# A staging place moved by 1088 words at the seam between an MLP's up and down projections

## The chip, the cores and the metric

The program runs on one core of one Trainium2 chip, as one launch. The metric is the device time in microseconds of one execution; the number compared is the median of several runs.

## The reference

The reference is one inference step of a two-layer hybrid decoder. It serves a prompt of 1024 tokens and a sample group of 8 x 8 = 64 tokens with shared weights, 1088 tokens in all, in float32. Layer 0 mixes tokens with a diagonal state-space model, layer 1 with attention over shared keys and values; both also attend to a memory. What matters here is the MLP that ends each layer:

```
def sqrelu_mlp(x, w_up, w_down):
    h = jax.nn.relu(x @ w_up)
    return (h * h) @ w_down
...
    h = h + sqrelu_mlp(rmsnorm(h, p["norm_mlp"][i]), p["w_up"][i], p["w_down"][i])
```

`x` has 1024 features (D_MODEL) and the hidden layer has 4096 (D_FF), so `w_up` is 1024 x 4096 and `w_down` 4096 x 1024.

## The kernel before, in words

The 1088 tokens are cut into four column chunks of 272 (`CN`). Every product is made of three float32r matmuls, on a high and a low half of each operand. `split(H, L, src)` makes such halves: the scalar engine writes the rounded high half (line 221), then the vector engine, or GpSimd, writes the difference (line 222).

**Strassen-like products.** The MLP multiplies 2 x 2 blocks with seven products instead of eight. `seven` (lines 428 to 455) runs them in order on TensorE, each into one of three pairs of PSUM banks in turn, so a product can start only when the readers of the product three places earlier are through. After product 4 it calls `out(1, 1, p, u4)` and then, on line 449, adds the same bank to `u2`; that line is the bank's last reader. `out` is given by the caller. In the up projection it is line 578 and squares the rectified sum; in the down projection it adds into the accumulator `H5` (line 627 for the first of the seven blocks of hidden features, 629 and 630 for later ones).

**The up projection.** `mlp` walks over sixteen pairs of up tiles in the order 14, 0 to 13, 15. Each leaves four results `q[m][n]` (hidden tile m, token half n). For tiles 0 to 13, `to_hidden` forms the seven operands that the down projection will need, splits each into a staging place and writes it to the DRAM scratch tensors `hops`. Tiles 14 and 15 belong to the eighth block of hidden features, which is multiplied in the conventional way at the end: there the four results are split as they are, in the order (0,0), (1,1), (0,1), (1,0), into the places of the list `hl4`, and written half by half to the scratch tensor `hcnv` (32 transfers over both layers). The transfers out of `hcnv`'s staging and the operand loads are tied into one issue order on SyncE's queue by `load_on`.

**The storage.** All of this lives in `setA`, four places of 2176 words (per partition). A ring of ten temporaries of 544 words (`tmps`) uses

```
((3, 0), (2, 0), (1, 1), (3, 1), (2, 1), (1, 2), (1, 3), (3, 2), (3, 3), (1, 0))
```

where (i, j) is words 544j to 544j + 543 of place i. Three staging places of 1088 words (`hl`) are the upper half of place 2 and the two halves of place 0. For the last tile the list `hl4` names four places, with the fourth outside that ring.

**The seam.** When the last up tile (15) is computed, the first down weights and the first four operands of block 0 are loaded; the other three operand loads are issued behind the first staged result (`late`). Then the down projection starts. Its accumulator `H5` covers all of `setA`:

```
H5 = joined(setA).at([128, 2, 2, 8, CN])
...
h = H5[:, :, n, 4 * d + 2 * e + m, :]
```

so that token half n and row r of the output lie at words 272r of places n and n + 2. The first down pair (block 0, d = 0) runs its two seven-product sequences interleaved and writes rows 0 to 3, words 0 to 1087 of every place; the second (d = 1) writes words 1088 to 2175. The down projection then goes on through blocks 1 to 6, with weights split on the fly into the eight places `wr`, which come free as TensorE finishes with them.

**The order of the work.** The source gives the engines and the traced order; the compiler's scheduler orders each engine's queue from the dependencies and a timing model, and derives the semaphore waits from which words overlap. So moving a place changes the waits, and can change the order on the queues.

Of the kernel before, what the change touches and what calls it, by code (L numbers as in the profile page):

```python
# [48 lines left out]
def yoco_step(ctx: ExitStack, tc: tile.TileContext, I, O, upto=99, dbg=None):  # L49
# [116 lines left out]
    setA = [top.words(n) for n in CW]  # L166
# [44 lines left out]
    def mm3(out, aH, aL, bH, bL, first, last):  # L211
        mm(out, aH, bH, first, False)
        mm(out, aH, bL, False, False)
        mm(out, aL, bH, False, last)
# [21 lines left out]
    def flush():  # L236
        while later:
            tick()
# [148 lines left out]
    def xop(i, g):  # L387
        return xplace[g][i].at([128, 2, 4, CN], F32R)
# [38 lines left out]
    def seven(lhs, rhs, nk, gs, tmp, out):  # L427

        s1, u2, u4 = (t[:, gs] for t in tmp)

        def product(i):
            n = turn["bank"] = (turn["bank"] + 1) % 3
            v = shaped(banks[:, 1024 * n:1024 * n + 1024], [128, 2, 512], F32)[:, :, 0:CN]
            for g in range(gs.start, gs.stop):
                for k in range(nk):
                    mm3(v[:, g], *lhs(i, k), *rhs(i, g, k), k == 0, k == nk - 1)
            return v[:, gs]

        S.activation(s1, product(0), AF.Copy)
        yield  # L440
        V.tensor_tensor(u2, product(1), s1, op=ALU.add)
        yield
        out(0, 0, product(2), s1)
        yield
        V.tensor_tensor(u4, product(3), u2, op=ALU.add)
        yield
        p = product(4)
        out(1, 1, p, u4)
        V.tensor_tensor(u2, p, u2, op=ALU.add)
        yield  # L450
        out(0, 1, product(5), u4)
        yield
        out(1, 0, product(6), u2)
        yield

    def by_turns(*seqs):
        for _ in zip(*seqs):
            tick()
# [45 lines left out]
    def mlp(l, hs, done, each=None):  # L504
# [6 lines left out]
        hl = Ring([setA[i].sub(1088 * j, 1088) for i, j in ((2, 1), (0, 0), (0, 1))])  # L511
        hl4 = [hl.p[i] for i in (0, 1, 2, 0)]
        late = []

        def up_weights(j, more=False):
            return weight_ops((I["w_up"][l, 2 * j:2 * j + 2].rearrange("m p k f -> p m k f"), [2, 8, 128]),
                              lambda r: (r[:, 0, 0:4], r[:, 0, 4:8], r[:, 1, 0:4], r[:, 1, 4:8]), [4, 128], more)
# [10 lines left out]
        def to_hidden(j, q):  # L528
            b, kp = j // 2, j % 2

            def put(i, x):
                t = hl([128, 2, 2, CN], F32R)
                split(t[:, 0], t[:, 1], x)
                SY.dma_start(out=hops[i][b][:, kp], in_=t.rearrange("p h g n -> p h (g n)").bitcast(F32))

            if b < 7:
                operands(q[0][0], q[0][1], q[1][0], q[1][1], tmps(sh), put)
                return
            for (m, n), place in zip(((0, 0), (1, 1), (0, 1), (1, 0)), hl4):
                t = place.at([128, 2, 2, CN], F32R)  # L540
                split(t[:, 0], t[:, 1], q[m][n])
                to = hcnv[2 * kp + m].rearrange("p h (g n x) -> p h g n x", g=2, n=2)
                for i in range(2):
                    load_on(to[:, i, :, n], t[:, i].bitcast(F32))
                if late:
                    load_operands(late.pop(0))

        def down_weights(b, d):
            return weight_ops((I["w_down"][l, b, 2 * d:2 * d + 2].rearrange("i p k f -> p i k f"), [2, 4, 256]),
                              lambda r: tuple(r[:, :, k:4:2, 128 * m:128 * m + 128] for m in range(2) for k in range(2)),  # L550
                              [2, 2, 128])

        def next_operands(b):

            t = [hring([128, 2, 2, 2 * CN], F32R) for _ in range(7)]
            r = [t[i] for i in (0, 5, 1, 6, 2, 3, 4)] if b == 0 else t

            def load(which):
                for i in which:
                    load_on(r[i].bitcast(F32), hops[i][b])  # L560

            return r, load
# [4 lines left out]
        for n, j in enumerate(jorder):  # L567
            take = tmps if n else first
            tmp = [take(sh) for _ in range(3)]
            q = [[take(sh) for _ in range(2)] for _ in range(2)]  # L570

            for gs in (slice(0, 1), slice(1, 2)) if n < 2 else (slice(0, 2),):
                if n == 0 and gs.start:
                    continue

                def out(m, n, ps, u):
                    x = q[m][n][:, gs]
                    V.tensor_tensor(x, ps, u, op=ALU.add)  # L578
                    S.activation(x, x, AF.Relu)  # L579
                    S.activation(x, x, AF.Square)  # L580

                by_turns(seven(lambda i, k: (W[i][:, 0, k, :], W[i][:, 1, k, :]),
                               lambda i, g, k: (xop(i, g)[:, 0, k, :], xop(i, g)[:, 1, k, :]), 4, gs, tmp, out))
            if n == 0:

                flush()
                for m, c in ((1, 0), (0, 0), (1, 1), (0, 1)):
                    turn["bank"] = (turn["bank"] + 1) % 3
                    ps = banks[:, 1024 * turn["bank"]:1024 * turn["bank"] + CN]
                    for i in range(2):  # L590
                        a, x = W[((0, 2), (7, 6))[m][i]], xop(((0, 2), (6, 5))[c][i], 1)
                        for k in range(4):
                            mm3(ps, a[:, 0, k, :], a[:, 1, k, :], x[:, 0, k, :], x[:, 1, k, :], i + k == 0, i + k == 4)
                    t = q[m][c][:, 1]
                    S.activation(t, ps, AF.Relu)
                    S.activation(t, t, AF.Square)
                held.pop()()
            if j < 15:
                W = up_weights(jorder[n + 1])
            else:  # L600
                W = down_weights(0, 0)
                ops, load_operands = next_operands(0)
                load_operands(range(4))
                late[:] = [(4, 5, 6)]
                hl4 = [hl.p[1], hl.p[0], hl.p[2], setA[1].sub(0, 1088)]
            to_hidden(j, q)


# [759 lines left out]
    def mlp0_done(h, c):  # L1368
# [10 lines left out]
        defer(4, rest)  # L1379

    mlp(0, hs, mlp0_done, add_square)
    if upto == 4:
        flush()
# [422 lines left out]
    def mlp1_done(h, c):  # L1806
# [16 lines left out]
        defer(4, rest)  # L1823

    mlp(1, hs, mlp1_done, add_square)
    flush()

# [113 lines left out]
```

## Time and profile before

| what | value |
|---|---|
| median of 3 runs | 2723.41 us (2720.01 to 2724.05) |
| the profiled execution: time, span | 2729.51 us, 2727.7 us |
| mean granted TensorE clock | 0.978 |
| TensorE matmul busy | 2564.0 us, 94% of the span |
| TensorE weight load busy | 2392.2 us, 88% |
| VectorE (DVE) busy | 1959.2 us, 72% |
| ScalarE (ACT) busy | 1256.6 us, 46% |
| GpSimd (POOL) busy | 1213.1 us, 44% |
| mean HBM traffic | 205 GB/s over the span |

The profiled execution is one run of its own, taken with the profiler on; it lies 6.1 us above the median of the timed runs. Times inside it are microseconds from the start of its span. Rows of the timeline read: start, duration, engine, source line, operation, what is written from what, shapes, how many, and in brackets the idle time before it with what ended that. PE is a matmul on TensorE, PEld its weight load, SPq an instruction of SyncE's queue. `banks` is PSUM, `plain` is the float32 storage that holds `setA`, `rounded`, `mlp` and `flexr` hold float32r operands, `flex` holds the temporaries of the down projection. Line numbers are mostly those of helpers, so lines 209, 221 and 222 (matmul and split) gather the work of the whole kernel. The seam of layer 0 lies at about 843 us, that of layer 1 at about 2341 us.

### The profile page before, as it was taken

How to read it: one execution, taken by the hardware profiler on the slowest of the kernel's cores; microseconds unless marked ns; L12 is line 12 of the kernel's file. 1: busy time of each engine (PE TensorE's matmuls, PEld its weight loads, DVE VectorE, ACT ScalarE, POOL GpSimd, SP SyncE). 2: the span in 40 equal slices, each digit the busy share in tenths (PEclk: the TensorE clock that was granted, in tenths of full speed). 3: DMA queues.
4: the chain of work that ended last, by engine and by line, in shares of the span. 5: the costliest groups of instructions: out<-in, count | busy, mean ns of one | idle time of the engine just before them, and what ended most of it. 6: DMA issues, size and time to landing. Idle time of an engine off the chain costs nothing.

```text
span 2727.7 us, 54053 instructions
## 1 busy us (share of the span) xinstructions
PE 2564.0 (94%) x20369; PEld 2392.2 (88%) x20369; DVE 1959.2 (72%) x3406; ACT 1256.6 (46%) x2612; POOL 1213.1 (44%) x1119
## 2 busy tenths in 40 slices
PE   6888899999998999999999999999989999899998
PEld 5777779899998999999889867777989999899998
DVE  8898665988886777794323278886588788677776
ACT  5433444566663222244322367775366665322224
POOL 4576310323321799842310455651032222179984
PEclk8999899999999999999999999999999999999999
DMA  6445352266558567443476889986226656866741
GB/s 200 106 104 146 117 163 76 91 242 243 229 228 324 232 254 277 178 167 102 150 259 222 268 290 308 304 294 218 91 87 244 236 227 234 318 242 244 285 169 67
DMA packets 242283, 561.66 MB, mean 206 GB/s; under 512 B 54053, under 2 KB 129382, under 8 KB 224614
## 3 DMA queue, kind: packets, MB, share of 16 engines
q1 hardware_dynamic: 212646, 548.50, 56.7%
q10 hardware_dynamic: 28864, 8.92, 1.4%
q8 instruction: 161, 2.64, 0.4%
q0 software_dynamic: 512, 0.79, 0.1%
q14 instruction: 100, 0.82, 0.1%
HBM read 386.19 MB, written 171.93 MB: 205 GB/s over the span
## 4 chain that ended last, share of the span: by engine, by line
PE 41%; DVE 18%; POOL 10%; DMA 10%; issue 6%; ACT 4%; SPq 0%; POOLq 0%; ACTq 0%; DVEq 0%
PE banks L209 39%; DMA hops<-plain 5%; DVE rounded L222 5%; POOL plain L630 4%; DVE plain L222 4%; PE banks L1667 1%; POOL plain L416 1%; DMA rounded<-hmid 1%; DVE plain L578 1%; POOL plain L646 1%; ACT plain L221 1%; POOL plain L422 1%; DMA hcnv<-plain 1%; POOL plain L417 1%; DMA plain<-fpast 1%
## 5 line engine op out<-in xcount | busy, mean ns | idle before, releaser
L209 PE MATMUL banks<-rounded 128*128 128x272 f32 (+3 forms) x11168 | 1552.6, 295 | 72.8 <-ACT rounded L221 18.3
L209 PEld LDWEIGHTS banks<-rounded 128*128 128x128 f32 x11168 | 1456.7, 191 | 120.3 <-ACT rounded L221 21.1
L221 ACT ACTIVATE rounded<-plain 128x512 fp32r<-128x512 f32 (+5 forms) x573 | 379.8, 676 | 637.5 <-PE banks L209 449.3
L222 DVE TENSOR_TENSOR rounded<-plain,rounded 128x512 fp32r<-128x512 f32 (+4 forms) x518 | 502.8, 976 | 121.7 <-ACT rounded L221 120.3
L209 PE MATMUL banks<-mlp,rounded 128*128 128x272 f32 x3816 | 516.8, 290 | 12.2 <-DVE plain L627 4.8
L209 PEld LDWEIGHTS banks<-mlp,rounded 128*128 128x128 f32 x3816 | 493.8, 189 | 17.2 <-DVE plain L627 5.3
L416 POOL TENSOR_TENSOR plain<-plain 128x512 f32<-128x512 f32 x60 | 103.9, 1731 | 705.9 <-DVE rounded L222 705.9
L630 POOL TENSOR_TENSOR plain<-plain,flex 128x544 f32<-128x544 f32 x192 | 289.8, 1520 | 37.7 <-DVE plain L629 34.8
L222 DVE TENSOR_TENSOR plain<-plain 128x544 fp32r<-128x544 f32 x212 | 171.1, 820 | 69.9 <-ACT plain L221 69.1
L221 ACT ACTIVATE plain<-plain 128x544 fp32r<-128x544 f32 x212 | 136.7, 650 | 111.6 <-DMA hops<-plain 99.1
L629 DVE TENSOR_TENSOR plain<-banks,plain 128x544 f32<-128x544 f32 x192 | 137.9, 718 | 50.3 <-PE banks L209 46.8
L422 POOL TENSOR_TENSOR plain<-plain 128x512 f32<-128x512 f32 x60 | 98.3, 1639 | 63.0 <-DVE rounded L222 62.6
L209 PE MATMUL banks<-flexr,rounded 128*128 128x272 f32 x816 | 114.5, 290 | 4.0 <-DVE flexr L222 4.0
L209 PE MATMUL banks<-layer 128*32 128x256 f32 (+3 forms) x1152 | 111.9, 368 | 5.5 <-DVE layer L1770 1.7
L579 ACT ACTIVATE plain<-plain 128x544 f32<-128x544 f32 (+1 forms) x136 | 83.2, 613 | 66.0 <-DVE plain L578 65.5
L209 PEld LDWEIGHTS banks<-flexr,rounded 128*128 128x128 f32 x816 | 107.8, 191 | 4.4 <-DVE flexr L222 4.4
L222 POOL TENSOR_TENSOR rounded<-plain,rounded 64x512 fp32r<-64x512 f32 (+2 forms) x55 | 77.9, 1424 | 67.1 <-ACT rounded L221 61.9
L222 POOL TENSOR_TENSOR rounded<-flex,rounded 128x544 fp32r<-128x544 f32 (+7 forms) x100 | 65.9, 668 | 83.7 <-ACT rounded L221 71.0
L578 DVE TENSOR_TENSOR plain<-banks,plain 128x544 f32<-128x544 f32 (+1 forms) x136 | 90.5, 666 | 11.8 <-PE banks L209 11.2
L222 DVE TENSOR_TENSOR rounded<-banks,rounded 128x512 fp32r<-128x512 f32 (+2 forms) x136 | 86.0, 637 | 13.1 <-ACT rounded L221 11.3
L221 ACT ACTIVATE rounded<-banks 128x512 fp32r<-128x512 f32 (+2 forms) x136 | 75.1, 559 | 42.0 <-PE banks L1667 29.3
L418 POOL TENSOR_TENSOR plain<-plain 128x512 f32<-128x512 f32 x60 | 91.7, 1528 | 2.8
(365 smaller groups left out, 3227.0 us busy)
## 6 DMA issues: line engine op xcount, KB each, us to landing
hops<-plain SPq DMA_DIRECT2D x196, 544.0 KB
rounded<-hops SPq DMA_DIRECT2D x66, 1088.0 KB
plain<-in_cache_kT SPq DMA_DIRECT2D x128, 384.0 KB
layer<-in_cache_v SPq DMA_DIRECT2D x128, 384.0 KB
mlp<-hops SPq DMA_DIRECT2D x32, 1088.0 KB
plain<-in_w_up SPq DMA_DIRECT2D x32, 1024.0 KB
plain<-in_w_down SPq DMA_DIRECT2D x28, 1024.0 KB
plain<-in_xT SPq DMA_DIRECT2D x8, 1088.0 KB
```

The lines of the kernel that those rows point to most:

```text
L209: PE.matmul(out, a, b, start=first, stop=last)
L221: S.activation(H, src, AF.Copy)
L222: return e.tensor_tensor(L, src, H.bitcast(F32), op=ALU.subtract)
L416: G.tensor_tensor(a22, a21, a22, op=ALU.add)
L417: G.tensor_tensor(a21, a11, a21, op=ALU.subtract)
L418: G.tensor_tensor(a11, a22, a11, op=ALU.subtract)
L422: G.tensor_tensor(a12, a12, a11, op=ALU.subtract)
L578: V.tensor_tensor(x, ps, u, op=ALU.add)
L579: S.activation(x, x, AF.Relu)
L629: V.tensor_tensor(h, ps, h, op=ALU.add)
L630: G.tensor_tensor(h, h, u, op=ALU.add)
L646: G.tensor_tensor(hc, hc, hr[:, m, :], op=ALU.add)
```

## The change

One line of `mlp`: the fourth place in `hl4` moves from words 0 to 1087 of place 1 to words 1088 to 2175 of the same place. It holds the split result (1,0) of up tile 15 until it has been written to `hcnv`. The new place is the storage of the results (0,0) and (0,1) of the same tile.

```
@@ -602,7 +602,7 @@
                 ops, load_operands = next_operands(0)
                 load_operands(range(4))
                 late[:] = [(4, 5, 6)]
-                hl4 = [hl.p[1], hl.p[0], hl.p[2], setA[1].sub(0, 1088)]
+                hl4 = [hl.p[1], hl.p[0], hl.p[2], setA[1].sub(1088, 1088)]
             to_hidden(j, q)
```

More of the change, by code (lines that the diff above doesn't have):

```diff
@@ L604, in mlp @@
                 late[:] = [(4, 5, 6)]
-                hl4 = [hl.p[1], hl.p[0], hl.p[2], setA[1].sub(0, 1088)]
+                hl4 = [hl.p[1], hl.p[0], hl.p[2], setA[1].sub(1088, 1088)]
             to_hidden(j, q)
```

## The prediction

> **What bounds the kernel now.** I read the page's chain of work first, then everything that touches the scratch tensor `hcnv` (the last up tiles' staged halves), and then the order in time around the first down pair. TensorE carries most of the chain, and one of its links is a transfer out of the staging:
>
> ```profile
> PE 41%; DVE 18%; POOL 10%; DMA 10%; issue 6%; ACT 4%; SPq 0%; POOLq 0%; ACTq 0%; DVEq 0%
> L526 SPq DMA_DIRECT2D hcnv<-plain x32: 359/448/3726, 529.1 to 2361.5; - x32
>   DVE plain L627: 11.2, 2
> 860.04 11.39 DMA hcnv<-plain
> 871.52 0.46 DVE plain L627
> 872.17 0.73 DVE flex L449
> ```
>
> The second and third lines are from the view of `hcnv`: 32 transfers, and who waited for them: two first-pair sums (L627), 11.2 us together, one per layer. The last three are the chain in layer 0: it runs through a staging transfer into L627 and from there through L449. In order of time (DVE, TensorE and DMA issues of layer 0; brackets give the idle time before and its releaser):
>
> ```profile
> 848.82 2.29 ACT L221 ACTIVATE plain<-plain 128x544 fp32r<-128x544 f32 x4
> 849.69 3.14 DVE L222 TENSOR_TENSOR plain<-plain 128x544 fp32r<-128x544 f32 x2
> 853.39 1.79 DVE L222 TENSOR_TENSOR plain<-plain 128x544 fp32r<-128x544 f32 x2
> 855.11 1.28 DVE L222 TENSOR_TENSOR rounded<-plain,rounded 128x512 fp32r<-128x512 f32 x2
> 855.66 1.46 SPq L526 DMA_DIRECT2D rounded<-hops x3
> 856.95 1.39 DVE L627 TENSOR_TENSOR plain<-banks,flex 128x544 f32<-128x544 f32 x2
> 857.16 7.25 SPq L526 DMA_DIRECT2D hcnv<-plain x6
> 857.71 3.09 PE L209 MATMUL banks<-mlp,rounded 128*128 128x272 f32 x12 [2.42 <-DVE plain L627]
> 861.47 4.74 PE L209 MATMUL banks<-rounded 128*128 128x272 f32 x36 [0.67 <-DMA rounded<-hops]
> 865.29 0.69 DVE L222 TENSOR_TENSOR rounded<-plain,rounded 128x512 fp32r<-128x512 f32 x1 [3.13 <-ACT rounded L221]
> 871.52 0.72 DVE L627 TENSOR_TENSOR plain<-banks,flex 128x544 f32<-128x544 f32 x1 [5.54 <-DMA hcnv<-plain]
> 872.17 0.71 DVE L449 TENSOR_TENSOR flex<-banks,flex 128x544 f32<-128x544 f32 x1
> 872.93 10.11 PE L209 MATMUL banks<-rounded 128*128 128x272 f32 x60 [6.72 <-DVE flex L449]
> 903.88 7.68 PE L209 MATMUL banks<-rounded 128*128 128x272 f32 x60
> 2369.88 0.72 DVE L627 TENSOR_TENSOR plain<-banks,flex 128x544 f32<-128x544 f32 x1 [5.61 <-DMA hcnv<-plain]
> 2371.28 10.16 PE L209 MATMUL banks<-rounded 128*128 128x272 f32 x60 [6.79 <-DVE flex L449]
> ```
>
> Read it from the matmuls backwards. TensorE stops at 861.47 + 4.74 = 866.21 and starts again at 872.93, because it needs the PSUM banks of an earlier product, whose last reader is L449. L449 stands on DVE right behind L627, and L627 is held 5.54 us by the staging transfer. Layer 1 repeats this within 0.1 us. There is a second loss behind the stall: 60 matmuls then take 10.11 us, where 60 of the same form take 7.68 us later on. The windows (columns: length, busy time and count of PE, weight load, DVE, ACT, POOL, then the granted clock) say why:
>
> ```profile
> 852.60:853.50 0.90, 0.00 (x0) 0.00 (x0) 0.90 (x3) 0.54 (x1) 0.90 (x1) 1.00 0.27 90
> 853.50:855.30 1.80, 1.76 (x12) 1.55 (x12) 1.80 (x3) 0.64 (x1) 0.47 (x1) 1.00 0.00 0
> 857.70:860.80 3.10, 3.09 (x12) 2.77 (x12) 0.63 (x1) 0.19 (x1) 0.00 (x0) 0.50 0.96 359
> 866.20:872.90 6.70, 0.01 (x1) 0.00 (x0) 1.38 (x3) 0.00 (x0) 0.00 (x0) 0.88 1.08 384
> 872.90:877.50 4.60, 4.57 (x20) 4.57 (x21) 3.20 (x5) 0.63 (x1) 0.00 (x0) 0.50 1.01 420
> 903.90:911.50 7.60, 7.60 (x63) 7.60 (x62) 4.25 (x6) 0.00 (x0) 4.11 (x4) 1.00 1.00 421
> ```
>
> After the long stall the clock is 0.50 for 4.6 us; after the idle 0.9 us at 852.6 it stays at 1.00.
>
> **The change, step by step.** In words of storage: the sums of the first down pair go to the first 1088 words of each of the four places of `setA`. Before, the fourth staged result (1,0) lies in words 0 to 1087 of place 1, so the sums there must wait until both its halves have left. After, it lies in words 1088 to 2175, which only the second pair writes. Nothing is added to or taken from any queue: the same splits, transfers and sums, with one place moved.
>
> *Removed: the wait of L627.* Two bounds per layer. If DVE's order stays as it is, L627 starts when the weight split before it ends, 865.29 + 0.69 = 865.98; L449 starts 0.65 us after it (872.17 - 871.52) and TensorE 0.76 us after that (872.93 - 872.17): 867.39 instead of 872.93, a gain of 5.54 us with 1.18 us of idle left. If L627 goes ahead of that weight split, it starts when its product ends, about 861.47 + 4.74 x 12/36 = 863.05, L449 is through by 864.4 and the stall of 6.72 us is gone. The order is worked out by the scheduler from dependencies; L627 is traced ahead of that split and came behind it only while it was waiting, so I take the second value: 6.72 us in layer 0 and 6.79 us in layer 1.
>
> *Removed with it: the slow clock.* 10.11 - 7.68 = 2.43 us, and 10.16 - 7.68 = 2.48 us in layer 1. It goes if the idle time left is short. Bounds: 0 recovered if what is left is as long as the 2.42 us before 857.71, which was followed by a clock of 0.50; all of it if it is like the 0.9 us at 852.6, which was not. What is left is 0 or 1.18 us, nearer to the latter; I take all. [...]
>
> *Moved: the fourth split.* Its new place is where results (0,0) and (0,1) of the same tile lie (the ring of ten temporaries stands at its third place when the last tile starts, so (0,0) and (0,1) come to lie at words 1088 and 1632 of place 1). So its scalar half must now wait until DVE has read (0,0), and its vector half writes over (0,1). In the queues as they are, the four run in the order (1,1), (1,0), (0,1), (0,0); now (1,0) has to be the last. In the rows: four scalar halves back to back from 848.82, four vector halves until 853.39 + 1.79 = 855.18. With (0,0) third, DVE has read it at about 854.5, the fourth scalar half ends at about 855.2, and the fourth vector half slips in behind a weight split. Behind it wait on DVE the weight splits and L627 of 856.95, and TensorE behind that. Cost: 0 if DVE has a weight split to do meanwhile (it has two, 855.11), 0.7 us if it idles for the scalar half instead, and about 0.9 us if the scalar half also holds ACT's next weight splits. On the other side, if the half is placed behind the two sums of 856.95, these come 0.64 us earlier. I take 0. The lower end: the whole earlier stall of 2.42 us and its slow clock (3.09 us against 12/60 of 7.68, so 1.55 us) go too, 4.0 us per layer.
>
> *Moved on SP: nothing.* Order on that queue is fixed for these transfers. The first staged result, (0,0), comes out earlier, so the three operand loads at 855.66 move up by at most 0.6 us; the fourth result's two transfers are the last of the six, ready long before their turn (split by about 856, issued from about 860).
>
> *What is late next.* The product after the stall needs the third of the loads issued at 855.66. The first held TensorE until 861.47; two more of 1088 KB follow in the queue, at these rates:
>
> ```profile
> 861.00:863.00 2.00, 1.53 (x12) 1.56 (x13) 1.16 (x2) 0.24 (x1) 0.00 (x0) 0.97 1.02 426
> 863.00:865.00 2.00, 2.00 (x18) 2.00 (x17) 0.00 (x0) 0.38 (x1) 0.00 (x0) 1.00 1.01 348
> 865.00:867.00 2.00, 1.21 (x10) 0.99 (x8) 0.69 (x1) 0.26 (x1) 0.00 (x0) 1.00 0.93 312
> 883.14 0.72 DVE L627 TENSOR_TENSOR plain<-banks,flex 128x544 f32<-128x544 f32 x1 [1.73 <-ACT flex L439]
> 887.58 0.72 DVE L627 TENSOR_TENSOR plain<-banks,flex 128x544 f32<-128x544 f32 x1 [0.78 <-PE banks L209]
> PE banks L209 <- DVE flex L441: 2.8, 3, 1.2
> PE banks L209 <- ACT rounded L221: 2.0, 3, 0.7
> PE banks L209 <- DVE rounded L222: 1.9, 5, 0.4
> PE banks L209 <- DVE flex L449: 0.8, 1, 0.8
> ```
>
> 2.23 MB at 0.85 + 0.70 + 0.62 MB per 2 us arrive by about 867.1. Without a stall that product starts at 866.21 + 1.5 = 867.7: in time, with 0.6 us to spare. The second pair's sums start at 883.14 and reach place 1's upper words at 887.58; about 9 us earlier still lies 7 us behind the last transfer (871.5). From 880 to 1130 TensorE waits only the 7.5 us of the last four rows, so it sets the pace and keeps what it gains; those waits follow its own progress.
>
> *The sum.* 6.72 + 2.43 + 6.79 + 2.48 = 18.4 us against the profiled execution's 2729.5 us (span 2727.7): 2711.1. The median of the runs is 6.1 us lower, 2723.4, so 2705. With DVE's order kept it is 5.54 + 2.43 + 5.61 + 2.48 = 16.1 us, 2707.3.
>
> **Rivals.** (a) *The third load takes over.* Its landing is bounded only by 861.47 and by 871.5, when a transfer queued behind it had landed. At the late bound TensorE idles 871.5 - 867.7 = 3.8 us and pays the 2.4 us of clock: 3.0 of 9.2 us remain per layer, 2717.5; halfway, some 5 us per layer, 2713. The rates above speak against it. (b) *The sums wait all the same*, because the tracker sees the strided sum as one long range, or what is gained waits for something later: 2723. Against it: the sums at 856.95 ran before the six transfers of 857.16 were even issued, four of which read upper words of the places that these sums write. (c) *Slower.* The queues' order is worked out anew from the changed dependency, in the whole down part. If there the weight splits (L221 and L222 on `rounded`) come behind the sums, TensorE waits for weights. It does so for 2.0 + 1.9 us per down part now; this decides the sign once it grows by more than 9.2 us in each layer, and at 15 us per layer the time is 2723.4 + 2 x (15 - 9.2) = 2735. For it: the schedule is free to move; against it: the weights' queue places are freed by TensorE's own progress, which only shifts.
>
> **How the numbers follow.** Changes under 0.2% (5.4 us) can't be told from none here. The forecast, stall and slow clock gone, 0.74, with a range of its own of 2701 to 2709 (2 us per layer off the earlier stall; or the kept order with 0.9 us per layer lost to the fourth split); (a) 0.11, mostly below 2718; (b) 0.09; (c) 0.06. The lower end is the earlier stall gone too, 18.4 + 8 = 26 us, 2697; the upper is (a) near its bound, 2716. Faster 0.83, same 0.11, slower 0.06.
>
> **What would show it.** Right: L627 waits for no `hcnv` transfer; the 6.7 us before L449's release shrink to under 1.3; the 60 matmuls after it take about 7.7 us at a clock of 1.00; ACT's group of four splits falls into three and one, the last after DVE. Wrong: TensorE waiting there for `rounded<-hops`, a longer stall before 857.7, the clock still 0.50 behind a short stall, or more waits on weight splits in the rest of the down part.

## The result, and the profile after

The changed kernel takes 2707.33 us (median of 5 runs, 2705.85 to 2710.51) against 2723.41 us before (5 runs, 2719.56 to 2726.01). The ratio is 0.9948, with a 95% interval of 0.9936 to 0.996. The forecast was 2705, with a range of 2697 to 2716. On two later occasions, beside other kernels, the ratio was 0.9924 (0.991 to 0.9937) and 0.9951 (0.9937 to 0.9965).

The page of the changed kernel, its span and its chain of work:

```profile
span 2708.7 us, 54049 instructions
PE 50%; DVE 14%; POOL 10%; DMA 7%; issue 5%; ACT 3%; SPq 0%; POOLq 0%; ACTq 0%; DVEq 0%
```

DMA's share of the chain fell from 10% to 7%, DVE's from 18% to 14%, and TensorE's rose from 41% to 50%. The view of `hcnv` (how many transfers, who waited for them):

```profile
L526 SPq DMA_DIRECT2D hcnv<-plain x32: 359/434/3462, 528.2 to 2349.6; - x32
  ACT plain L221: 1.2, 1
  DVE plain L222: 0.6, 1
```

L627, which waited 11.2 us in two places, is no longer in the list. The seam in order of time (first one row of before, then layer 0 of the changed kernel, then its two matmul rows of layer 1):

```profile
852.51 0.63 ACT L221 ACTIVATE rounded<-plain 128x512 fp32r<-128x512 f32 x1 [1.40 <-PE banks L209]
851.85 1.74 ACT L221 ACTIVATE plain<-plain 128x544 fp32r<-128x544 f32 x3
857.61 0.66 ACT L221 ACTIVATE plain<-plain 128x544 fp32r<-128x544 f32 x1 [4.02 <-DVE plain L222]
858.18 1.13 ACT L221 ACTIVATE rounded<-plain 128x512 fp32r<-128x512 f32 x2
860.79 1.34 DVE L627 TENSOR_TENSOR plain<-banks,flex 128x544 f32<-128x544 f32 x2
861.55 1.77 PE L209 MATMUL banks<-mlp,rounded 128*128 128x272 f32 x12 [3.23 <-DVE plain L627]
863.58 10.74 PE L209 MATMUL banks<-rounded 128*128 128x272 f32 x84 [0.26 <-DMA rounded<-hops]
865.35 0.72 DVE L627 TENSOR_TENSOR plain<-banks,flex 128x544 f32<-128x544 f32 x1 [0.67 <-PE banks L209]
865.99 0.72 DVE L449 TENSOR_TENSOR flex<-banks,flex 128x544 f32<-128x544 f32 x1
868.13 0.68 DVE L222 TENSOR_TENSOR rounded<-plain,rounded 128x512 fp32r<-128x512 f32 x1
2345.70 3.09 PE L209 MATMUL banks<-mlp,rounded 128*128 128x272 f32 x12 [3.23 <-DVE plain L627]
2348.59 12.03 PE L209 MATMUL banks<-rounded 128*128 128x272 f32 x84
```

The 84 matmuls that were cut in two by the stall of 6.72 us now run through. L627 at 865.35 waits only for its product and stands ahead of the weight split (868.13) that it used to follow. What is new is the idle time of 4.02 us on ACT: the fourth split waits for DVE, and two weight splits come behind it. Counted from the seam's first matmul group (843.32 us before, 846.35 after, below), the first of them starts 11.8 us in (858.18) instead of 9.2 (852.51).

How much the seam alone gained shows from its first matmul group to the first reload of `hcnv` near the end of the same MLP. Before (the first and third row are TensorE's, the others SyncE's):

```profile
843.32 3.27 PE L209 MATMUL banks<-rounded 128*128 128x272 f32 x24 [0.94 <-DVE plain L449]
1118.86 3.33 SPq L651 DMA_DIRECT2D mlp<-hcnv  x3
2341.55 3.27 PE L209 MATMUL banks<-rounded 128*128 128x272 f32 x24 [1.15 <-DVE plain L449]
2617.36 4.83 SPq L651 DMA_DIRECT2D mlp<-hcnv  x4
```

After:

```profile
846.35 3.26 PE L209 MATMUL banks<-rounded 128*128 128x272 f32 x24 [0.97 <-DVE plain L449]
1113.18 4.82 SPq L651 DMA_DIRECT2D mlp<-hcnv  x4
2330.49 3.27 PE L209 MATMUL banks<-rounded 128*128 128x272 f32 x24 [0.59 <-DVE plain L449]
2598.47 4.82 SPq L651 DMA_DIRECT2D mlp<-hcnv  x4
```

275.54 us became 266.83 in layer 0, 275.81 became 267.98 in layer 1: 8.7 and 7.8 us, 16.5 together. The two spans differ by 19.0 us; the rest, some 2.5 us, lies outside the seams (layer 0's seam starts 3.0 us later than before, layer 1's 11.1 us earlier). Such shifts come and go between profiles: from the reload of layer 0 to the seam of layer 1 the changed kernel took 1217.3, 1222.4 and 1218.9 us in its three profiles (before: 1222.7), while the two intervals from seam to reload gained 16.5, 16.2 and 16.4 us. So the interval from seam to reload is the better measure.

### The profile page after: what moved, and what is told of

Same layout as the page of the kernel before. It is cut to its first block, busy times and chain, and to the rows that moved or that the text cites. A ratio compares the mean times of both kernels' runs of the same rounds, so it can differ in the third digit from the quotient of the medians.

```text
span 2708.7 us, 54049 instructions
## 1 busy us (share of the span) xinstructions
PE 2556.0 (94%) x20369; PEld 2386.3 (88%) x20369; DVE 1956.5 (72%) x3406; ACT 1256.5 (46%) x2612; POOL 1213.0 (45%) x1119
## 4 chain that ended last, share of the span: by engine, by line
PE 50%; DVE 14%; POOL 10%; DMA 7%; issue 5%; ACT 3%; SPq 0%; POOLq 0%; ACTq 0%; DVEq 0%
PE banks L209 48%; DVE rounded L222 4%; POOL plain L630 4%; DMA hops<-plain 3%; DVE plain L222 2%; POOL plain L416 1%; DMA rounded<-hmid 1%; PE banks L1667 1%; POOL plain L646 1%; POOL plain L422 1%; POOL plain L417 1%; DVE plain L578 1%; ACT rounded L221 1%; ACT plain L221 1%; POOL plain L1293 1%
## 5 line engine op out<-in xcount | busy, mean ns | idle before, releaser
L416 POOL TENSOR_TENSOR plain<-plain 128x512 f32<-128x512 f32 x60 | 106.2, 1770 | 685.3 <-DVE rounded L222 685.3
L422 POOL TENSOR_TENSOR plain<-plain 128x512 f32<-128x512 f32 x60 | 97.9, 1632 | 64.3 <-DVE rounded L222 63.8
L209 PE MATMUL banks<-rounded,layer 128*128 128x256 f32 x480 | 89.8, 300 | 2.7 <-ACT rounded L221 2.5
```

Of the source, the lines that this page charges most:

```text
L209: PE.matmul(out, a, b, start=first, stop=last)
L416: G.tensor_tensor(a22, a21, a22, op=ALU.add)
L422: G.tensor_tensor(a12, a12, a11, op=ALU.subtract)
```

## Experiments

Of each edit only the lines that matter are shown, shortened with `...`; a line with a minus is one of the changed kernel.

**The changed kernel again.** No edit.

> The changed kernel again, beside the others on one chip. Theory (the wait of L627 for the fourth staging's transfers is gone, and with it the slow clock behind it): 14 to 19 us under before, L627 waits for no hcnv transfer. Whether the half clock follows the remaining stall of 3.2 us was different in its two layers (1.77 us for 12 matmuls in layer 0, 3.09 us in layer 1); if that depends on where the stall falls in a window that runs freely, this run may show it the other way round or in both.

2703.87 us against 2724.05, 20.2 us less where 19 was the most expected, ratio 0.9924 (0.991 to 0.9937), and `hcnv` holds no L627. In layer 0 its twelve matmuls behind the first stall took this:

```profile
856.59 3.09 PE L209 MATMUL banks<-mlp,rounded 128*128 128x272 f32 x12 [3.23 <-DVE plain L627]
859.47 2.92 PE L209 MATMUL banks<-rounded 128*128 128x272 f32 x12
```

The same stall of 3.23 us that left the clock alone in layer 0 of the first profile (1.77 us) halved it here. So whether it is followed by the slow clock varies from run to run. The profiles of these two runs of the changed kernel (two stalls each) and that of the kernel with the change in layer 0 alone hold five stalls of this length: behind four of them the twelve matmuls ran at half clock (0.50, 0.50 and 0.51 in the windows, 3.05 us instead of 1.77 in the last), behind one at 1.00. How busy TensorE was around them is told under the slow clock, further down.

**The old place, its transfers sent early.** The storage overlap stays; the fourth result's transfers leave third and fourth instead of seventh and eighth. No engine's queue changes its order.

```
-for (m, n), place in zip(((0, 0), (1, 1), (0, 1), (1, 0)), hl4):
+for (m, n), place in zip(((0, 0), (1, 0), (1, 1), (0, 1)) if j == 15 else ..., hl4):
...
+hl4 = [hl.p[1], setA[1].sub(0, 1088), hl.p[0], hl.p[2]]
```

> The old place, but the fourth result's two transfers go out as the third and fourth of the eight instead of last; the queues of all five engines keep the order of before. Theory (L627 waits for just that transfer): its wait falls from 5.5 to about 2 us per layer (the first transfer behind the operand loads instead of the fifth), TensorE's stall from 6.7 to about 3.2 us, 7 to 12 us under before, 2711 to 2716. Rival (the gain of the change is one of queue order, not of the wait): the time of before, within 2 us.

2714.46 us, 9.6 us under before, ratio 0.996 (0.9946 to 0.9973): as expected by the theory of the wait. `hcnv` holds L627 for 1.9 us in two places instead of 11.2, and layer 0 shows the shorter stall:

```profile
  DVE plain L627: 1.9, 2
871.61 0.72 DVE L627 TENSOR_TENSOR plain<-banks,flex 128x544 f32<-128x544 f32 x1 [1.12 <-DMA hcnv<-plain]
873.02 9.29 PE L209 MATMUL banks<-rounded 128*128 128x272 f32 x60 [2.29 <-DVE flex L449]
```

This shows the wait as the cause without any new order: about half of the gain comes from sending the transfers in another sequence. The stall is 2.3 us instead of 6.7, and the 60 matmuls behind it still take 9.29 us, not 7.68 (in layer 1: 1.9 and 7.76 us). From seam to reload the two layers gain 9.1 us.

**Half of the overlap.** Words 544 to 1631, so that rows 0 and 1 of the pair's sums are free and rows 2 and 3 are not.

```
-hl4 = [..., setA[1].sub(1088, 1088)]
+hl4 = [..., setA[1].sub(544, 1088)]
```

> The fourth place at words 544 to 1631 of place 1: rows 0 and 1 of the first pair's sums are free of it, rows 2 and 3 still wait for the transfer of its scalar half. Theory (a sum waits exactly for the half that lies under it): the first sum of the interleaved pair waits for no hcnv transfer, the second, a matmul product later, still does; the stall falls from 6.7 to some 3 to 4 us and 3 to 9 us of the whole are gained, 2715 to 2721. Rival (any overlap with the pair holds all of it): the time of before.

2717.17 us against 2726.14, ratio 0.9958 (0.9944 to 0.9973). The sums behave row by row (DVE, then TensorE, layer 0):

```profile
864.74 0.72 DVE L627 TENSOR_TENSOR plain<-banks,flex 128x544 f32<-128x544 f32 x1 [0.45 <-PE banks L209]
873.19 0.73 DVE L627 TENSOR_TENSOR plain<-banks,flex 128x544 f32<-128x544 f32 x1 [2.65 <-DMA hcnv<-plain]
874.60 7.26 PE L209 MATMUL banks<-rounded 128*128 128x272 f32 x35 [3.89 <-DVE flex L449]
```

A free sum goes ahead while a later one waits 2.65 us, and TensorE's stall is 3.89 us. The gain, 9.0 us between the medians, is at the top of what was expected; in the one profile the seams account for 6.2 us of it. The first stall, 3.8 us in both layers, takes in the one of 0.9 us that stands ahead of it before the change and after, and the half clock follows it in both.

**Layer 0 alone.**

```
+hl4 = [..., setA[1].sub(1088 if l == 0 else 0, 1088)]
```

> The change in layer 0 alone; the queues also get the changed kernel's other order at the start of layer 1's up projection. Theory (each seam gains by itself, some 8 to 10 us): half of the gain, 7 to 11 us under before, 2713 to 2717, and layer 1 keeps its stall of 6.8 us behind L449. Rival (a good part comes from the order at the start of layer 1's up projection): more than 11 us under before.

2716.62 us against 2726.14, ratio 0.9968 (0.9957 to 0.998), 9.5 us less and about half of the whole. In its profile, layer 0 has the 84 matmuls in one piece and layer 1 keeps its stall, at 5.48 us instead of the expected 6.8:

```profile
858.09 10.79 PE L209 MATMUL banks<-rounded 128*128 128x272 f32 x84
2350.92 10.27 PE L209 MATMUL banks<-rounded 128*128 128x272 f32 x60 [5.48 <-DVE flex L449]
```

From seam to reload layer 0 gains 8.3 us and layer 1 0.2. Each seam gains by itself. The changed kernel's other order at the start of layer 1's up projection, which this kernel has too, brings nothing that could be seen. The runs scatter widely (2708.89 to 2724.16 in 12 runs), and the interval leaves room for some 3 us either way.

**The fourth place in operand storage.** `setC[0]` is read by the last up tile and next filled after the first block.

```
-hl4 = [hl.p[1], hl.p[0], hl.p[2], setA[1].sub(1088, 1088)]
+hl4 = [hl.p[1], hl.p[0], hl.p[2], setC[0].sub(0, 1088)]
```

> The fourth place lies in setC[0], which neither the last tile's results nor the first pair's sums use. Theory (only the overlap with the first pair's sums costs; the new place adds 0.8 us per layer because its scalar half waits for the reading of (0,0)): the stall before L449 stays away, the first stall falls back from 3.23 to about 2.4 us, some 1.6 us under the changed kernel, 2704 to 2707. Rival (the time comes from the new order of the queues at the start of layer 1's up projection, which this kernel does not have): no better than about 5 us under before, 2718.

2709.57 us, ratio 0.9944 (0.9929 to 0.9959). It lacks the other order in layer 1's up projection and still gains 14.5 us, 14.2 of them from seam to reload, so that rival falls. The first stall did fall to 2.4 us, but the time did not follow: beside it on the same chip the changed kernel took 2703.87 us, so this one was 5.7 us slower, not 1.6 faster. TensorE now waits for the operand loads:

```profile
852.62 2.67 PE L209 MATMUL banks<-mlp,rounded 128*128 128x272 f32 x12 [2.42 <-DVE plain L627]
856.44 12.34 PE L209 MATMUL banks<-rounded 128*128 128x272 f32 x84 [1.14 <-DMA rounded<-hops]
2346.62 6.24 PE L209 MATMUL banks<-rounded 128*128 128x272 f32 x48 [2.53 <-DMA rounded<-hops]
```

These loads are issued behind the first staged result, (0,0), which comes last out of the four splits again. What the splits gave, the loads took.

**Two, then four results in operand storage.**

```
+hl4 = [setC[0].sub(1088, 1088), hl.p[0], hl.p[2], setC[0].sub(0, 1088)]
```

> As e1, and the first place, of result (0,0), lies in setC[0] too, so that (0,0) need not wait for the last operand transfer out of the staging ring and no sum of the first pair touches a staging place. Theory: (0,0) is split some microseconds earlier, DVE has one staging half less to do before the first sums, and the first stall shrinks from 3.2 to under 2 us; 2 to 8 us under the changed kernel, 2699 to 2706. Rival (DVE's load before the sums is the same, only earlier, and the stall is set by the splits of weights): as e1.

2707.24 us, ratio 0.993 (0.9915 to 0.9944). The first stall was 2.7 us in both layers, not under 2, with a second of 1.8 us in layer 1, and the time was above what was expected: 3.4 us over the changed kernel beside it, not 2 to 8 under.

```
+hl4 = [setC[0].sub(0, 1088), setC[3].sub(0, 1088), setC[0].sub(1088, 1088), setC[3].sub(1088, 1088)]
```

> All four staged results of the last tile lie in operand storage that is free by then (two in setC[0], two in setC[3]), so no split waits for the ring's transfers and no sum for a staging transfer. Theory (what is left of the seam's loss is the stall before the first sums, 3.2 us and the slow clock that follows it in some runs, set by what DVE has to do before them): the stall shrinks to 1 to 2.7 us, and the time is 0 to 6 us under the changed kernel, 2698 to 2706. Rival (that stall is set by the weight splits on DVE and GpSimd alone): no better than the kernel with two results in setC[0], 2705 to 2709.

2701.99 us, ratio 0.9915 (0.9899 to 0.9932). The stall of 3.23 us and the one of 0.95 ahead of it become two, of 1.3 and 1.8 us. In layer 0 of this profile no slow stretch follows; in layer 1 (last two rows) one does, and the 60 matmuls take 9.02 us:

```profile
853.14 1.77 PE L209 MATMUL banks<-rounded 128*128 128x272 f32 x12 [1.28 <-DVE flex L445]
856.76 1.76 PE L209 MATMUL banks<-mlp,rounded 128*128 128x272 f32 x12 [1.84 <-DVE plain L627]
858.36 7.67 PE L209 MATMUL banks<-rounded 128*128 128x272 f32 x60
2335.38 1.99 PE L209 MATMUL banks<-mlp,rounded 128*128 128x272 f32 x12 [1.80 <-DVE plain L627]
2337.17 9.02 PE L209 MATMUL banks<-rounded 128*128 128x272 f32 x60
```

**The same, with two halves on GpSimd.**

```
+split(t[:, 0], t[:, 1], q[m][n], G if j == 15 and (m, n) in ((0, 0), (1, 1)) else V)
```

> As e6, with the difference halves of results (0,0) and (1,1) made on GpSimd, which idles some 14 us before the seam, instead of on DVE. Theory (DVE's load is what holds the first sums): two halves, 1.4 us or more, less on DVE, the stall under 1.5 us, 1 to 4 us under e6. Rival (GpSimd's weight steps come later for it and hold the splits): 0 to 4 us slower than e6.

2701.93 us, ratio 0.9916 (0.9895 to 0.9937): no different from the version before it, where 1 to 4 us less were expected. DVE's load is not what is left of the second of the two stalls; L627 waits there for another transfer (1.5 to 1.7 us for `hops<-plain`), which reads the staging ring under the pair's sums.

**Changed kernel and best version side by side.**

> The changed kernel beside the version with four results in operand storage, on one chip. 14 to 20 us under before; its seams keep a stall of 3.2 us, followed by the full clock or the half clock, as the window falls.

> All four staged results of the last tile in setC[0] and setC[3], again, now beside the changed kernel. Theory (the seam is 1 to 3 us shorter per layer, its stalls being 1.3 and 1.8 us and followed by no long stretch of half clock): 2 to 6 us under the changed kernel. Rival (what the seams gain is less than what runs differ by): within 1 us of the changed kernel.

2709.90 us (0.9951, 0.9937 to 0.9965) and 2701.97 us (0.9916, 0.9902 to 0.993). The intervals do not meet: on this occasion four results in operand storage beat the change by some 8 us between the medians, which is more than was expected. In the two profiles the seams account for 3.0 us of it (19.4 us gained from seam to reload against 16.4; the other two profiles with four results there gained 21.8 and 23.2), though the profiled execution was the fastest of its five for the changed kernel and the slowest of its five for the other. Where the rest comes from was not settled, and it may not last: on the first occasion the changed kernel's median, 2703.87 us, was only 2 us above these.

## Why the prediction was right

*The bound and the wait.* Right. The overlap of the fourth place with the first pair's sums held L627, L449 behind it, and TensorE behind that; moving the place, half of it, or only its transfers' turn scales the stall from 6.7 to 0, 3.9 and 2.3 us.

*L627 goes ahead of the weight split.* Right: 865.35 before 868.13. So the whole stall went, not only 5.5 us of it.

*The slow clock goes with it.* Right in layer 0: 84 matmuls in 10.74 us, the full rate. In layer 1 they took 12.03 us, because the half clock behind the first stall reaches into them. The term was tied to the wrong measure. The prediction took idle times near 1 us as harmless and 2.4 us as harmful; the traces show no such threshold. In the clock records of the profiles before and after, all changes of the granted clock lie whole multiples of 3.4133 us apart (to 0.005 us); 17 of the stretches at half clock last one such step, 11 last two. Windows cut at the edges of these steps, with the prediction's columns and then the DMA share and GB/s (one of before, two of layer 0 after the change, four of layer 1):

```profile
854.28:857.69 3.41, 1.01 (x9) 0.79 (x7) 3.41 (x7) 0.36 (x1) 1.59 (x1) 1.00 0.50 135
856.59:860.01 3.42, 1.73 (x12) 1.51 (x12) 2.69 (x4) 1.70 (x3) 0.64 (x2) 1.00 0.47 122
860.01:863.42 3.41, 1.77 (x12) 1.55 (x12) 2.18 (x5) 0.18 (x1) 1.35 (x1) 1.00 0.98 388
2341.39:2344.81 3.42, 1.08 (x9) 0.86 (x7) 2.69 (x5) 1.70 (x3) 0.89 (x1) 1.00 0.61 168
2344.81:2348.22 3.41, 2.52 (x11) 2.52 (x12) 1.47 (x3) 0.00 (x0) 0.70 (x1) 0.50 1.04 431
2348.22:2351.64 3.42, 3.42 (x17) 3.42 (x17) 1.42 (x3) 0.63 (x1) 0.00 (x0) 0.50 1.02 377
2351.64:2355.05 3.41, 3.41 (x29) 3.41 (x29) 3.15 (x6) 0.63 (x1) 0.00 (x0) 1.00 0.96 317
```

What went with the clock here is how busy TensorE was in a step. In layer 0 an edge (860.01) cut the stall of 3.23 us in two, both steps were just over half busy (1.73 and 1.77 us), and the clock stayed at 1.00. In layer 1 the same stall fell mostly into one step, 32% busy (1.08 us), and the next two steps ran at 0.50. Before the change, the stall of 2.42 us fell into one step, 30% busy (1.01 us), and the half clock followed.

The four seams of the two profiles hold nine steps at full clock in which TensorE was less than 60% busy (the profile's PE column). Behind those of 0, 0, 29, 30 and 32% the clock was 0.50, behind those of 45, 50, 51 and 52% it stayed at 1.00. Near one half the share alone did not settle it: far ahead of the seams, at 151.13, 205.75 and 267.19 us of the profile before, steps of 47, 47 and 52% were followed by 0.50. So the full clock behind the first stall of layer 0 was luck: of the five stalls of 3.23 us, only this one, which an edge cut in the middle, kept it.

The long stall of before held one step with no matmul at all (867.94 to 871.35) and was followed by two at half clock (871.35 to 878.17), the first of which still held the end of the stall. 5.2 us of matmuls fell into these two (1.82 and 3.41), and the 60 matmuls took 2.4 us longer than at 1.00 (10.11 instead of 7.68).

*The fourth split.* This is the term that was mis-sized. The prediction took 0 between bounds of a gain of 4.0 and a loss of 0.9 us per layer. Its scalar half was placed ahead of ACT's next two weight splits, ACT idled 4.02 us before it, the first of the two started 2.6 us later than before, and the first stall grew from 2.42 to 3.23 us in both layers: 0.8 us each, almost the bound. So two of the prediction's own signs of being wrong did appear: a longer stall before the first sums and, in layer 1, the clock of 0.50 behind it. In layer 0 the clock made that good by luck (1.77 us instead of 3.09), in layer 1 it did not.

*What is late next.* Right in kind: the loads were in time, with 0.26 us of waiting. They are close behind, as the fourth place in `setC[0]` shows, where the same loads cost 1.1 and 2.5 us.

*Kept to the end.* Nearly. In the rest of layer 0's down projection TensorE's waits, 7.5 us before, are now

```profile
PE banks L209 <- DVE flex L441: 2.8, 3, 1.2
PE banks L209 <- DVE rounded L222: 2.6, 6, 0.8
PE banks L209 <- DVE flex L449: 1.4, 2, 0.7
PE banks L209 <- ACT rounded L221: 1.3, 2, 0.7
PE banks L209 <- DVE plain L629: 0.7, 1, 0.7
```

8.8 us: 1.3 us given back to a new order.

*The sum.* Forecast 18.4 us, 9.2 per seam; measured 16.5 us over the seams and 16.1 us between the medians. In layer 0 the rows add up: 6.72 + 2.43 for the stall and its clock, less 0.81 for the longer first stall, plus 1.32 for its clock, plus 0.41 for the load, less 1.3 given back, is 8.8 us, against 8.7. In layer 1 two more rows of before are needed:

```profile
2355.94 2.93 PE L209 MATMUL banks<-mlp,rounded 128*128 128x272 f32 x12 [2.43 <-DVE plain L627]
2359.75 4.75 PE L209 MATMUL banks<-rounded 128*128 128x272 f32 x36 [0.88 <-DVE flex L445]
```

There it is 6.79 + 2.48, less 0.80 for the longer first stall, less 0.16 (3.09 instead of 2.93) and 1.29 (12.03 instead of 10.74) for the half clock behind it, plus 0.88 for a wait that is gone, less some 0.4 given back later: 7.5 us, against 7.8. That the total came out 2 us under the forecast is therefore the sum of a mis-sized split, a clock that fell well in one layer and badly in the other, and small waits, not one term.

*The rivals.* (b) and (c) did not come about. (a) did not decide here, but is the next thing in line.

## What to carry to other kernels

When an accumulator reuses storage from which results are still being sent, the words that its first sums touch should be those whose transfers are done first; either move the place or move its transfers forward. Follow the waiting instruction to what stands behind it on its engine: a sum that waits 5.5 us cost TensorE 9 us, because the reader that frees its bank stood next in line and the clock fell behind the stall. A place that is free of one wait can carry another (here the reading of the results it overwrites), so look for storage that nobody near needs.

## What was not expected of the hardware

The granted clock behind an idle time of 2.4 to 3.2 us is not a function of that time: 1.00 or 0.50 for the same 3.23 us in the two layers of one run, and 3.09 or 1.77 us for the same twelve matmuls. The stall that lay mostly in one step of 3.4133 us (32% busy) had half clock behind it; the one that an edge split over two steps (51 and 52% busy) had not. So the price of a stall of this length differs from run to run with the place of the steps. The same point of the same program (the twelve matmuls behind the first stall of layer 0) lies at 861.55 us in one profile of the changed kernel and at 856.59 us in another, so an effect of a few microseconds is better read over an interval inside the profile than from the span.
